# Two-layer hybrid backbone in one kernel: fewer filler matmuls in the first stage, a last block output by output, and shifted places in the order of three later parts

## The chip, the cores and the metric

The kernel runs on one core of a Trainium2 chip. The metric is the device time of one execution in microseconds (us); lower is better. The kernel before was run three times: 1451.67, 1452.0 and 1443.84 us, median 1451.67. One more execution was recorded by the profiler; all durations below come from that one.

The engines are named as in the profile: PE is TensorE (matmuls; PEld is its weight load, the step that puts the stationary operand into the array), DVE is VectorE, ACT is ScalarE, POOL is GpSimd, and SP is SyncE, which issues most of the loads. Each engine works through its own list of instructions in order and waits on semaphores for the others.

## What is computed

Two layers over 256 latent tokens and 256 context tokens of width 1024, all in float32. Each layer has a token mixer with three branches (retention, neighbourhood attention, grouped-query attention) and an MLP, both with RMS norms that are modulated by vectors computed from a conditioning input. The last layer only gives latent tokens.

```python
for l in range(DEPTH):
    last = l == DEPTH - 1
    mod_lat = (silu_c @ w_mod[l] + b_mod[l])[:, None, :]
    mod_ctx = silu_cc @ w_mod[l] + b_mod[l]
    sh1, sc1, gt1, sh2, sc2, gt2 = jnp.split(mod_lat, 6, axis=-1)
    ...
    h = rms_norm(x, g_pre_mix[l]) * (1.0 + sc1) + sh1
    hc = rms_norm(ctx, g_pre_mix[l]) * (1.0 + csc1) + csh1
    y, yc = token_mixer(h, hc, w_in[l], ...)
    x = x + gt1 * rms_norm(y, g_post_mix[l])
    h = rms_norm(x, g_pre_mlp[l]) * (1.0 + sc2) + sh2
    x = x + gt2 * rms_norm(squared_relu_mlp(h, w_mlp_in[l], w_mlp_out[l]), g_post_mlp[l])
    if not last:
        ...
```

Inside the mixer the grouped-query branch normalises each query head, so it needs the mean of the squares of every 64 query columns (`rms_norm(heads(gq, 8), q_gain)`).

## The kernel before, in words

**Precision and weight tiles.** Every product is made from three matmuls. A weight tile of 128x1024 floats arrives as `wr`. ACT rounds it to `wh` (the hi part), DVE subtracts to get `wl` (the lo part); `wsplit` (L230) does this and `mm3` (L184) issues hi by hi, hi by lo, lo by hi. The activations are split the same way into `hT` (layer input, transposed) or `u` (MLP hidden). There are three buffers each of `wr`, `wh` and `wl` (L34, L35). Functions `ahead` and `cut` (L1432 to L1451) issue loads three tiles ahead and splits two tiles ahead of the step that uses them.

**Who sets the order.** `MANUAL` is False (L26), so a scheduler sets the order of the instructions on each engine. It starts from the order in which the code issues them, which is a list of steps put together at L1371 to L1419. Only the prologue and a few marked steps are kept in program order (class `Ordered`, L61). The order on an engine is fixed at build time; on the chip nothing overtakes there.

**First stage** (`prologue`, L243). It computes the first two modulation vectors of layer 0, the normalised and transposed input `hT`, and the first projection (`rq`, `rk`; outputs `pr0` to `pr3`), for pairs of 128-row blocks called 0 to 3. Its order is a string, `PLAN` (L51), whose words `go` (L345) reads: `A00` are the matmuls on `modps` with the first weight tile of block 0, one word for each of its four tiles (`a2` for all four at once); `r` copies the row out of PSUM on ACT; `f` turns it into columns (the `pm` matmuls on PE and six small DVE steps, `sh` and `sc`); `T` and `t` are the transpositions `ph` of the input; `h` scales, shifts and splits them into `hT` (ACT, then DVE); `c` and `d` split the weight tile (ACT, DVE: `pwh`, `pwl`); `Gkm` is one of the six groups of four matmuls (over the four outputs) that block k adds; `w8` are eight filler matmuls of 128x128 zeros into `pr3`, whose result is overwritten. Ahead of all that, `init` (L277) issues `WARM` matmuls of 128x512 zeros. In the profile each of these float32 matmuls shows as two passes. The twenty `pr` tiles of 512 KB are issued on SP one after the other (L255), five to a block: tiles 0 to 3 for `A`, tile 4 for `G`. POOL copies one element of tile 14 (`late`, L262) and only then issues its own loads.

**Layer-0 MLP** (`mlp_steps`, L1220). First come projections of 256 columns (steps `m1`) for seven of the eight hidden chunks of the latent tokens (s0), mixed with the preparation of the context tokens' `hT` (`pre_steps`, L573), then the same seven for the context tokens (s1), and one projection of 512 columns for the eighth chunk. Then come eight steps of the second product (`pO`, four PSUM outputs, evicted by DVE into `z`), and the same for three more quarters. Each weight tile serves one step.

**Modulation by DVE** (`mod_dve`, L429). The other modulation vectors are summed on DVE: a tile `mr` of 128x1024 weights is loaded by POOL (two buffers), and for each stream (latent, context) one instruction `acc` multiplies it by a column and adds it up. A vector takes eight `mr` tiles, so 16 `acc` for both streams, and two finishing steps (`ahi`, `alo`, and for the gates `pg` matmuls and `G`). `weave_steps` (L1359) spreads such steps evenly between the steps of the main work. For the layer-0 MLP it takes the main steps from `MLA` = 16 to i - `MLB`, with i = 76 (the place where the last quarter is divided), L1383 to L1386: 60 fill steps over steps 16 to 65.

**Grouped-query branch** (`gq_done`, L1032). After each of four projections, ACT squares the result (`gsq`), PE sums the squares by tiny matmuls (`gqm`), DVE copies the sums (`qms`), then `rope` rotates the query. After the fourth, DVE makes the reciprocal roots. `mid` (L594) is called in the middle of a projection and runs what was put off to there. `NB2` (L33, L1391) is the number of layer-1 mixer steps that are issued between the normalisation of the context tokens and their transpositions.

Of the kernel before, what the change touches and what calls it, by code (L numbers as in the profile page):

```python
# [21 lines left out]
EPS = 1e-6  # L22
# [4 lines left out]
NS = 31  # L27
M0A = -28
M0B = -2
MLA = 16  # L30
MLB = 10
NT = 8
NB2 = 5  # L33
WR = 3  # L34
WH = 3  # L35
WLD = 3
# [11 lines left out]
END = ((0, 0), (1, 0))  # L48
ORD = ((0, 4, 5), (0, 4, 8))
FILL = (((0, 9), (9, 21), (21, 33)), ((0, 9), (7, 22), (22, 39)))  # L50
PLAN = ("A00 w8 A01 w6 T00 A02 w6 A03 r0 b0 w4 f0 T01 c0 w10 h00 d0 h01 w8 "  # L51
# [4 lines left out]
GATE = 14  # L56
PAD, PAD2, WP = 424, 272, 1152
WARM = 5


class Ordered:  # L61
# [20 lines left out]
def kernel(  # L82
# [26 lines left out]
    v_, s_, t_ = Ordered(tc, nc.vector), Ordered(tc, nc.scalar), Ordered(tc, nc.tensor)  # L109
# [18 lines left out]
    st = {}  # L128
# [16 lines left out]
    def T(name, w=512):  # L145
        return tp.tile([128, w], F32, tag="t", name=name)

    def sm(name, *shape):
        return smp.tile([128, *shape], F32, tag=name, name=name)
# [4 lines left out]
    def att(name="pa"):  # L154
        return atp.tile([128, 512], F32, tag="at", name=name)
# [4 lines left out]
    def ts(o, i, s1, s2, o0, o1):  # L160
        v_.tensor_scalar(out=o, in0=i, scalar1=s1, scalar2=s2, op0=o0, op1=o1)

    def tt(o, a, b, op):
        return v_.tensor_tensor(out=o, in0=a, in1=b, op=op)

    def stt(o, a, s, b, o0, o1):
        v_.scalar_tensor_tensor(out=o, in0=a, scalar=s, in1=b, op0=o0, op1=o1)
# [9 lines left out]
    def rsqrt(y, v, a):  # L177
        ts(y.bitcast(I32), v.bitcast(I32), -0.5, 1597463007.0, ALU.mult, ALU.add)
        for _ in range(3):
            stt(a, y, -0.5, v, ALU.mult, ALU.mult)  # L180
            tt(a, a, y, ALU.mult)
            stt(y, a, 1.5, y, ALU.add, ALU.mult)

    def mm3(ps, a, b, first, last):  # L184
        (ah, al), (bh, bl) = a, b
        t_.matmul(ps, ah, bh, start=first, stop=False)
        t_.matmul(ps, ah, bl, start=False, stop=False)
        t_.matmul(ps, al, bh, start=False, stop=last)
# [11 lines left out]
    sel = const.tile([128, 20], F32, tag="sel", name="sel")  # L200
# [42 lines left out]
    def prologue():  # L243
# [3 lines left out]
        pr = []  # L247
        M = {}
        raw, hi, rdy = {}, {}, {}
# [23 lines left out]
        def bias():  # L273
            M["b16"] = T("b16")
            nc.gpsimd.dma_start(out=M["b16"][0:16, 0:128], in_=b_mod[0, 0:2 * D].rearrange("(r n) -> r n", n=128))

        def init():  # L277

            w, zero = att("warm"), T("zero")
            v_.memset(zero, 0.0)  # L280
            for _ in range(WARM):
                t_.matmul(w, zero[:, 0:128], zero, start=True, stop=True)
# [20 lines left out]
        def early():  # L303
            for n_ in ("sh1", "sc1"):
                st[0, n_] = smp.tile([128, 8, 2], F32, tag=n_, name=n_, bufs=2)
            pr.extend(mmt(f"pr{i}") for i in range(4))
# [30 lines left out]
        def gemm(kp, u):  # L337
# [3 lines left out]
            for c in range(4):  # L341
                t_.matmul(pr[c], rdy[kp][i][:, k, 128 * c:128 * c + 128], hpair(kc, 512)[j],
                          start=(kc == 0 and u == 0), stop=(kc == 7 and u == 5))

        def go(ws):  # L345
            Ordered.on = True
            load_x(4)
            bias()
            load()
            init()  # L350
            early()
            sq = [pre_sq(0)]
            pre_xn(0, sq[0], True)
            sq.append(pre_sq(1))
            pre_xn(1, sq[1], True)
            ph, h32 = {}, {}
            for c in PLAN.split():
                o, n, m = c[0], int(c[1]), int(c[2:] or 0)
                if o == "c":
                    cast(n)  # L360
                elif o == "d":
                    cut(n)
                elif o == "A":
                    mod(n, (m,))
                elif o == "a":
                    mod(n)
                elif o == "r":
                    row(n)
                elif o == "w":
                    run_on(int(c[1:]))  # L370
                elif o == "b":
                    bias_columns()
                elif o == "T":
                    ph[n, m] = pre_tr(n, m)
                elif o == "t":
                    for s in range(2):
                        ph[n, s] = pre_tr(n, s)
                elif o == "f":
                    fin(n)
                elif o == "h":  # L380
                    for s in range(2):
                        if m == 0:
                            h32[s] = T("h32")
                        pre_h(0, 0, n, s, ph[n, s], (m,), h32[s])
                elif o == "G":
                    gemm(n, m)
            Ordered.on = False
            with tc.issue_after(st["hold"].ins), tc.issue_after(st["late"].ins):
                setup2()
            for i in range(4):  # L390
                st["qkdone"](i, pr[i])
# [165 lines left out]
    def pre_h(l, which, kp, s, pt, js=(0, 1), h32=None):  # L557
        sh, sc = ("sh1", "sc1") if which == 0 else ("sh2", "sc2")
        A, B = st[l, sc], st[l, sh]
        if h32 is None:  # L560
            h32 = T("h32")
        for j in js:
            kc = 2 * kp + j
            if s == 0:
                st["hT"][kc] = HL("hT", 256 if l and which else 512)
            h = st["hT"][kc]
            c = slice(256 * s, 256 * s + 256)
            i = slice(256 * j, 256 * j + 256)
            s_.activation(h32[:, i], pt[:, i], AF.Identity, scale=A[:, kc, s:s + 1], bias=B[:, kc, s:s + 1])
            v_.tensor_copy(h[0][:, c], h32[:, i])  # L570
            tt(h[1][:, c], h32[:, i], f(h[0][:, c]), ALU.subtract)
# [11 lines left out]
    def load_x(ntb):  # L583
        if "X" not in st:
            st["X"] = []
        for tb in range(len(st["X"]), ntb):
            X = S("X", F32)
            src = x if tb < 2 else xc
            r = 128 * (tb % 2)
            nc.sync.dma_start(out=X, in_=src[r:r + 128, :].rearrange("p (a b) -> p a b", a=2))  # L590
            st["X"].append(X)


    def mid():  # L594

        for u in st.pop("mid", ()):
            u()

    def hpair(kc, n):
        h = st["hT"][kc]  # L600
        return (h[0][:, 0:n], h[1][:, 0:n])
# [318 lines left out]
    def mixer(l):  # L920
        last = l == 1
        n = 256 if last else 512
# [109 lines left out]
        def gq_done(c):  # L1032
            def done(ps):
                if c == 0:
                    st["qms"] = smp.tile([128, 4, 8], F32, tag="qms", name="qms")
                sq = T("gsq")
                s_.activation(sq[:, 0:n], ps[:, 0:n], AF.Square)
                q = T("gq32")
                s_.activation(q[:, 0:n], ps[:, 0:n], AF.Copy, scale=gq_gain[:, 2 * l:2 * l + 1])
                pm = att("gqm")  # L1040
                for tb in range(n // 128):
                    t_.matmul(pm[:, 2 * tb:2 * tb + 2], sq[:, 128 * tb:128 * tb + 128], sel[:, 16:18], start=True, stop=True)
                v_.tensor_copy(st["qms"][:, 0:n // 128, 2 * c:2 * c + 2],
                               pm[:, 0:n // 64].rearrange("p (t e) -> p t e", e=2))
                rope(q)
                o = HL("gq", n)
                for e in range(2):
                    a, b = slice(64 * e, 64 * e + 64), slice(64 - 64 * e, 128 - 64 * e)
                    s_.copy(o[e][a], q[a, 0:n])
                    tt(o[e][b], q[a, 0:n], f(o[e][a]), ALU.subtract)  # L1050
                st.setdefault("gq", []).append(o)
                if c == 3:
                    w = n // 16
                    qm = st["qms"].rearrange("p t e -> p (t e)")
                    y, a = sm("gq_y", 4, 8), sm("gq_a", 32)
                    yf = y.rearrange("p t e -> p (t e)")
                    v_.tensor_scalar_add(out=qm[:, 0:w], in0=qm[:, 0:w], scalar1=EPS)
                    rsqrt(yf[:, 0:w], qm[:, 0:w], a[:, 0:w])
                    v_.tensor_scalar_mul(out=yf[:, 0:w], in0=yf[:, 0:w], scalar1=0.125)
                    st["qsc"] = y  # L1060
            return done

        for c in range(4):
# [310 lines left out]
    a, b = M0A, M0B  # L1374
# [7 lines left out]
    i = ml.index(None)  # L1382
    a, b = MLA, i - MLB  # L1383
    steps += ml[:a]
# [5 lines left out]
    m1_ = mixer(1)  # L1390
    steps += pc[:1] + m1_[:1 + NB2]  # L1391
    steps += pc[1:]
    steps += [([], lambda ws: st.__setitem__("X", st["X"][0:2]))]
    steps += m1_[1 + NB2:]
    steps += wout_steps(1, 0)
# [158 lines left out]
```

## Time and profile before

| what | value |
|---|---|
| runs | 1451.67, 1452.0, 1443.84 us (median 1451.67) |
| profiled execution | 1449.71 us |
| its span | 1448.0 us |
| mean granted TensorE clock | 0.995 of full speed |
| PE busy | 1420.2 us, 98% |
| DVE busy | 1049.8 us, 72% |
| ACT busy | 723.0 us, 50% |
| POOL busy | 75.7 us, 5% |
| HBM read | 217.22 MB |

The span is what the profile's engines cover; the execution's own time is 1.7 us longer. Busy shares are averages over stages that differ. A matmul's start is exact while its end is modelled, so the time that one takes in a row is best read from the start of the next. In the views, `ps<-hT,wh` means an instruction that writes a tile `ps` and reads `hT` and `wh`; the square brackets at the end of a row tell how long the engine stood idle before it and what released it. The line is L73 for nearly all, since a helper issues them, so tiles are told apart by name.

### The profile page before, as it was taken

What the parts mean: (1) busy time and instruction counts of PE and PEld (TensorE: products, weight loads), DVE (VectorE), ACT (ScalarE), POOL (GpSimd) and SP (SyncE); (2) the same over time, 40 slices, a digit from 0 to 9 for tenths busy, and PEclk for the clock granted to TensorE, in tenths of its full rate; (3) what the DMA queues carried; (4) which work ended last, traced back from release to release, by engine and by line L of the source; (5) the groups of instructions that cost most, each with busy time, mean ns of one, the idle gap of its engine ahead of it and who ended that gap; (6) DMA issues with size and microseconds to landing.
All of it is one profiled execution on the core that took longest, in us unless ns stands there. A gap on an engine that the chain in (4) does not pass through costs nothing.

```text
span 1448.0 us, 21148 instructions
## 1 busy us (share of the span) xinstructions
PE 1420.2 (98%) x8061; PEld 1206.5 (83%) x8061; DVE 1049.8 (72%) x1993; ACT 723.0 (50%) x1231; POOL 75.7 (5%) x139
## 2 busy tenths in 40 slices
PE   8999999999999999999999999999999999999997
PEld 6778788777888789988888678878889999899886
DVE  4767687777995879885855645986867886767544
ACT  3455366545322358524334144764646664487542
POOL 2000000000110000110110100000000000000000
PEclk9999899999999999999999999999999999999999
DMA  9332131222565566755673744533233446478653
GB/s 358 136 88 73 30 88 59 69 84 81 183 201 154 180 229 174 233 171 178 201 234 124 243 129 158 150 114 89 78 97 103 146 136 190 116 201 272 201 187 129
DMA packets 231862, 219.65 MB, mean 152 GB/s; under 512 B 7548, under 2 KB 188860, under 8 KB 231760
## 3 DMA queue, kind: packets, MB, share of 16 engines
q1 hardware_dynamic: 217568, 169.90, 37.8%
q0 software_dynamic: 13904, 47.88, 10.7%
q8 instruction: 63, 1.03, 0.3%
q10 hardware_dynamic: 288, 0.52, 0.1%
q14 instruction: 39, 0.32, 0.1%
HBM read 217.22 MB, written 1.05 MB: 151 GB/s over the span
## 4 chain that ended last, share of the span: by engine, by line
PE 82%; DVE 8%; DMA 5%; ACT 2%; issue 2%; SPq 0%; DVEq 0%; POOL 0%; ACTq 0%; POOLq 0%
PE ps L73 40%; PE pO L73 13%; PE br L73 7%; PE pB L73 6%; DMA mr<-in_w_mod_dram 4%; PE po L73 3%; PE pt L73 2%; DVE wl L73 2%; PE pr L73 2%; PE sl L73 2%; PE gkv L73 2%; DVE acc L73 1%; DVE hT L73 1%; PE ro L73 1%; ACT wh L73 1%
## 5 line engine op out<-in xcount | busy, mean ns | idle before, releaser
L73 PE MATMUL ps<-hT,wh 128*128 128x256 f32 (+1 forms) x2480 | 602.8, 335 | 3.5 <-DVE z L73 2.6
L73 ACT CAST wh<-wr 128x1024 fp32r<-128x1024 f32 x295 | 310.2, 1053 | 453.7 <-PE ps L73 180.6
L73 DVE TENSOR_TENSOR wl<-wr,wh 128x1024 fp32r<-128x1024 f32 x295 | 359.9, 1222 | 210.6 <-ACT wh L73 206.4
L73 PEld LDWEIGHTS ps<-hT,wh 128*128 128x128 f32 x2480 | 418.5, 190 | 58.2 <-issue 10.0
L73 PE MATMUL ps<-hT,wl 128*128 128x256 f32 (+1 forms) x1240 | 412.4, 333 | 1.1 <-DVE wl L73 1.1
L73 PEld LDWEIGHTS ps<-hT,wl 128*128 128x128 f32 x1240 | 234.2, 189 | 24.7 <-DVE wl L73 2.1
L73 PE MATMUL pO<-wh,u 128*128 128x512 f32 x768 | 239.4, 390 | 0.8 <-DVE z L73 0.8
L73 PEld LDWEIGHTS pO<-wh,u 128*128 128x128 f32 x768 | 144.2, 188 | 33.2 <-issue 2.6
L73 DVE SCALAR_TENSOR_TENSOR acc<-mr,cs,acc 128x1024 f32<-128x1024 f32 x112 | 140.7, 1281 | 32.4 <-DMA mr<-in_w_mod_dram 32.1
L73 PE MATMUL pO<-wl,u 128*128 128x512 f32 x384 | 149.6, 390 | 0.0
L73 PEld LDWEIGHTS pO<-wl,u 128*128 128x128 f32 x384 | 72.1, 188 | 14.7
L73 PE MATMUL pB<-wh,hT 128*128 128x512 f32 x256 | 82.4, 392 | 0.8 <-ACT rqk L73 0.8
L489 POOL DMA_DIRECT2D mr<-in_w_mod_dram x80 | 42.5, 531 | 426.7 <-DVE acc L73 403.8
L73 PE MATMUL pO<-wh,yT 128*128 128x512 f32 x192 | 59.7, 390 | 0.0
L73 PEld LDWEIGHTS pB<-wh,hT 128*128 128x128 f32 x256 | 48.1, 188 | 11.0 <-ACT rqk L73 1.2
L73 DVE TENSOR_TENSOR PT<-pt,PT 128x512 fp32r<-128x512 f32 x80 | 51.5, 683 | 2.4 <-ACT PT L73 1.7
L73 PE MATMUL pB<-wl,hT 128*128 128x512 f32 x128 | 50.0, 390 | 0.0
L73 ACT CAST PT<-pt 128x512 fp32r<-128x512 f32 x80 | 43.3, 599 | 8.9 <-PE pt L73 5.0
L73 DVE TENSOR_TENSOR u<-rl,u 128x256 fp32r<-128x256 f32 (+1 forms) x71 | 36.7, 518 | 12.4 <-ACT u L73 12.2
L73 PE MATMUL pt<-ident,P 128*128 128x128 f32 x320 | 41.6, 273 | 0.6 <-DVE P L73 0.6
L73 PEld LDWEIGHTS pO<-wh,yT 128*128 128x128 f32 x192 | 35.9, 188 | 7.3
L845 POOL DMA_DIRECT2D bt<-in_relb_dram x16 | 8.6, 540 | 628.7 <-DVE m L73 628.7
(273 smaller groups left out, 1849.6 us busy)
## 6 DMA issues: line engine op xcount, KB each, us to landing
wr<-in_w_m_dram SPq DMA_DIRECT2D x143, 512.0 KB, 4.4
wr<-in_w_in_dram SPq DMA_DIRECT2D x104, 512.0 KB, 3.7
mr<-in_w_mod_dram POOLq DMA_DIRECT2D x80, 512.0 KB, 4.2
wr<-in_w_br_dram SPq DMA_DIRECT2D x24, 512.0 KB, 3.5
wr<-in_w_out_dram SPq DMA_DIRECT2D x24, 512.0 KB, 4.1
pr<-in_w_mod_dram SPq DMA_DIRECT2D x16, 512.0 KB, 8.6
bt<-in_relb_dram POOLq DMA_DIRECT2D x16, 192.0 KB, 2.7
X<-in_x_dram SPq DMA_DIRECT2D x4, 512.0 KB, 4.7
```

What stands on the lines that cost most here:

```text
L73: ins = call(*a, **k)
L489: nc.gpsimd.dma_start(out=w, in_=w_mod[l, 128 * kc:128 * kc + 128, vec * D:vec * D + D].rearrange("p (a n) -> p a n", a=2))
L845: nc.gpsimd.dma_start(out=bt, in_=relb[l, h])
```

## The change

1. `PLAN`: fillers of block 0 go from 8, 6, 6, 4, 10 and 8 to 3, 2, 3, 2, none and 7 (42 to 17); `WARM` goes from 5 to 4.
2. The last three groups of block 3 become a word `L3`: the new `gemm_end` issues the same twelve matmuls output by output, so that `pr0` is complete first.
3. `MLA` goes from 16 to 8 and `MLB` from 10 to 6: the weave of the layer-0 MLP covers the main steps 8 to 69.
4. `NB2` goes from 5 to 6.
5. The square sums of the grouped-query branch (`gqm` matmuls, the copy into `qms`, after the fourth the roots) become a function `sums`, which the next call of `mid` runs.

```diff
-MLA = 16
-MLB = 10
+MLA = 8
+MLB = 6
 NT = 8
-NB2 = 5
+NB2 = 6
...
-PLAN = ("A00 w8 A01 w6 T00 A02 w6 A03 r0 b0 w4 f0 T01 c0 w10 h00 d0 h01 w8 "
+PLAN = ("A00 w3 A01 w2 T00 A02 w3 A03 r0 b0 w2 f0 T01 c0 h00 d0 h01 w7 "
...
-        "G30 G31 G32 G33 G34 G35")
+        "G30 G31 G32 L3")
...
-WARM = 5
+WARM = 4
...
+        def gemm_end(kp):
+
+            for c in range(4):
+                w = [x[:, 1, 128 * c:128 * c + 128] for x in rdy[kp]]
+                mm3(pr[c], w, hpair(2 * kp + 1, 512), False, True)
...
+                elif o == "L":
+                    gemm_end(n)
...
-        for u in st.pop("mid", ()):
+        for u in st.pop("late_mm", []) + list(st.pop("mid", ())):
             u()
...
-                pm = att("gqm")
-                for tb in range(n // 128):
-                    t_.matmul(pm[:, 2 * tb:2 * tb + 2], sq[:, 128 * tb:128 * tb + 128], sel[:, 16:18], start=True, stop=True)
-                v_.tensor_copy(st["qms"][:, 0:n // 128, 2 * c:2 * c + 2],
-                               pm[:, 0:n // 64].rearrange("p (t e) -> p t e", e=2))
                 rope(q)
...
+                def sums():
+                    pm = att("gqm")
...
+                st.setdefault("late_mm", []).append(sums)
```

What stands in an engine's list, place by place. First PE at the start of the kernel, before:

```order
L73 MATMUL warm<-zero 128x512 x5
L73 MATMUL modps<-pr,csz 32x256 x4
L73 MATMUL pr_192<-csz 128x128 x8
L73 MATMUL modps<-pr,csz 32x256 x4
L73 MATMUL pr_192<-csz 128x128 x6
L73 MATMUL ph<-ident,X 128x128 x4
L73 MATMUL modps<-pr,csz 32x256 x4
L73 MATMUL pr_192<-csz 128x128 x6
L73 MATMUL modps<-pr,csz 32x256 x4
L73 MATMUL pr_191<-ident,b_129 128x16
L73 MATMUL pr_192<-csz 128x128 x4
L73 MATMUL pm<-csz,r_283 128x2 x4
```

And of the change:

```order
L73 MATMUL warm<-zero 128x512 x4
L73 MATMUL modps<-pr,csz 32x256 x4
L73 MATMUL pr_191<-csz 128x128 x3
L73 MATMUL modps<-pr,csz 32x256 x4
L73 MATMUL pr_191<-csz 128x128 x2
L73 MATMUL ph<-ident,X 128x128 x4
L73 MATMUL modps<-pr,csz 32x256 x4
L73 MATMUL pr_191<-csz 128x128 x3
L73 MATMUL modps<-pr,csz 32x256 x4
L73 MATMUL pr_190<-ident,b_129 128x16
L73 MATMUL pr_191<-csz 128x128 x2
L73 MATMUL pm<-csz,r_270 128x2 x4
```

The row `pr<-csz` is a run of fillers. Each run is shorter, and the rows between stand in the same order.

Next DVE in the layer-0 MLP, from the first weight split after the last `hT` of the context tokens. `acc<-mr` is a modulation sum, `wl<-wr,wh` a weight split, `u<-rl` a split of the hidden activations. Before:

```order
L73 TENSOR_TENSOR wl_5633<-wr_5594,wh_5632 128x1024
L73 TENSOR_TENSOR u_5563<-rl_5589,u_5563 128x256
L73 TENSOR_TENSOR wl_5669<-wr_5630,wh_5668 128x1024
L73 TENSOR_TENSOR u_5293<-rl_5625,u_5293 128x256
L73 SCALAR_TENSOR_TENSOR acc_5779<-mr_5774,cs_103,brow_5776 128x1024
L73 TENSOR_TENSOR u_5330<-rl_5661,u_5330 128x256
L73 TENSOR_TENSOR wl_5705<-wr_5666,wh_5704 128x1024
L73 SCALAR_TENSOR_TENSOR acc_5781<-mr_5774,cs_103,brow_5776 128x1024
L73 TENSOR_TENSOR wl_5741<-wr_5702,wh_5740 128x1024
L73 TENSOR_TENSOR u_5367<-rl_5697,u_5367 128x256
L73 SCALAR_TENSOR_TENSOR acc_5779<-mr_5819,cs_103,acc_5779 128x1024
L73 TENSOR_TENSOR wl_5786<-wr_5738,wh_5785 128x1024
```

And of the change:

```order
L73 TENSOR_TENSOR wl_5628<-wr_5585,wh_5627 128x1024
L73 SCALAR_TENSOR_TENSOR acc_5524<-mr_5519,cs_103,brow_5521 128x1024
L73 SCALAR_TENSOR_TENSOR acc_5526<-mr_5519,cs_103,brow_5521 128x1024
L73 SCALAR_TENSOR_TENSOR acc_5524<-mr_5540,cs_103,acc_5524 128x1024
L73 SCALAR_TENSOR_TENSOR acc_5526<-mr_5540,cs_103,acc_5526 128x1024
L73 TENSOR_TENSOR u_5550<-rl_5576,u_5550 128x256
L73 TENSOR_TENSOR u_5267<-rl_5616,u_5267 128x256
L73 TENSOR_TENSOR u_5304<-rl_5656,u_5304 128x256
L73 TENSOR_TENSOR wl_5668<-wr_5625,wh_5667 128x1024
L73 SCALAR_TENSOR_TENSOR acc_5524<-mr_5581,cs_103,acc_5524 128x1024
L73 SCALAR_TENSOR_TENSOR acc_5526<-mr_5581,cs_103,acc_5526 128x1024
L73 SCALAR_TENSOR_TENSOR acc_5524<-mr_5621,cs_103,acc_5524 128x1024
```

Before, one `acc` at most stands between two `wl`; with the change four `acc` stand there, from the first `wl` on, for three tiles running (the third four follow after the last row shown here, then two, `u` and two).

Last PE in the same stretch. `ps<-hT,wh` and `ps<-hT,wl` are matmuls of a projection with the hi and the lo part of its weight tile. Before, at the end of one projection and the beginning of the next:

```order
L73 MATMUL ps_5708<-hT_5062,wh_5668 128x256 x2
L73 MATMUL ps_5708<-hT_5062,wl_5669 128x256
L73 MATMUL ps_5708<-hT_5066,wh_5668 128x256 x2
L73 MATMUL ps_5708<-hT_5066,wl_5669 128x256
L73 MATMUL ps_5744<-hT_5020,wh_5704 128x256 x2
L73 MATMUL ps_5744<-hT_5020,wl_5705 128x256
L73 MATMUL ps_5744<-hT_5024,wh_5704 128x256 x2
L73 MATMUL ps_5744<-hT_5024,wl_5705 128x256
```

And of the change, at the end of the projection that uses the first `wl` above:

```order
L73 MATMUL ps_5671<-hT_5040,wl_5628 128x256
L73 MATMUL ps_5711<-hT_4994,wh_5667 128x256 x2
L73 MATMUL ps_5751<-hT_4994,wh_5707 128x256 x2
L73 MATMUL ps_5791<-hT_4994,wh_5747 128x256 x2
L73 MATMUL ps_5711<-hT_4994,wl_5668 128x256
L73 MATMUL ps_5711<-hT_4998,wh_5667 128x256 x2
L73 MATMUL ps_5711<-hT_4998,wl_5668 128x256
L73 MATMUL ps_5711<-hT_5008,wh_5667 128x256 x2
```

With the change PE issues the first two hi matmuls of three projections before the first matmul that needs the second `wl`; the rest of each projection stands behind it in PE's order. On SP the order is the same in both; in layer 1 the projection issued ahead by `NB2` stands on PE where it stood.

## Rows read from the trace of the kernel before

**Rows 1.** The page, part 1: engine, busy us (share of the span), instructions.
```profile
PE 1420.2 (98%) x8061; PEld 1206.5 (83%) x8061; DVE 1049.8 (72%) x1993; ACT 723.0 (50%) x1231; POOL 75.7 (5%) x139
```

**Rows 2.** What PE waited for over the span: us in total, times, longest.
```profile
PE warm L73 <- DVE zero L73: 3.7, 1, 3.7
PE ph L73 <- ACT z L73: 3.3, 3, 1.6
PE ps L73 <- DVE z L73: 2.6, 2, 2.4
...
PE ps L73 <- DVE wl L73: 1.1, 2, 0.7
PE pO L73 <- DVE z L73: 0.8, 2, 0.5
...
PE pB L73 <- ACT rqk L73: 0.8, 1, 0.8
```

**Rows 3.** Busy time by engine (x instructions), PEclk, DMA share, GB/s, 582.3 to 596.6 us.
```profile
582.30:596.60 14.30, 14.30 (x121) 14.30 (x121) 12.43 (x14) 9.57 (x17) 1.08 (x2) 1.00 0.81 241
```

**Rows 4.** Timeline, 0 to 50 us: start us, us, engine, line, operation [idle before <- releaser].
```profile
8.11 0.34 PEld L73 LDWEIGHTS warm<-zero 128*128 128x128 f32 x1 [0.52 <-issue]
...
9.44 0.19 PEld L73 LDWEIGHTS warm<-zero 128*128 128x128 f32 x1 [0.24 <-issue]
...
11.20 0.64 PE L73 MATMUL modps<-pr,csz 128*32 128x256 f32 x8 [0.31 <-DVE pv L73]
...
11.77 2.05 PE L73 MATMUL pr<-csz 128*128 128x128 f32 x16
...
18.40 0.64 PE L73 MATMUL modps<-pr,csz 128*32 128x256 f32 x8
...
20.12 0.95 PE L73 MATMUL pm<-csz,r 128*128 128x2 f32 x8
...
21.40 4.18 PE L73 MATMUL pr<-csz 128*128 128x128 f32 x36
...
23.22 0.43 DVE L73 TENSOR_TENSOR hT<-h,hT 128x256 fp32r<-128x256 f32 x1
...
25.34 2.09 PE L73 MATMUL pr<-hT,pwh 128*128 128x512 f32 x8
...
30.65 0.18 POOL L262 COPY late<-pr 128x1 f32<-128x1 f32 x1 [27.16 <-DMA pr<-in_w_in_dram]
...
45.95 1.93 PE L73 MATMUL modps<-pr,csz 128*32 128x256 f32 x32
```

**Rows 5.** Timeline of DVE, 585 to 597 us.
```profile
586.16 1.28 DVE L73 SCALAR_TENSOR_TENSOR acc<-mr,cs,brow 128x1024 f32<-128x1024 f32 x1
587.36 1.22 DVE L73 TENSOR_TENSOR wl<-wr,wh 128x1024 fp32r<-128x1024 f32 x1
588.49 0.42 DVE L73 TENSOR_TENSOR u<-rl,u 128x256 fp32r<-128x256 f32 x1
588.83 1.28 DVE L73 SCALAR_TENSOR_TENSOR acc<-mr,cs,acc 128x1024 f32<-128x1024 f32 x1
```

**Rows 6.** Tile `mr`, 580 to 630 us: its last line.
```profile
DMA to landing us min/median/max: 3.8/4.3/7.2
```

**Rows 7.** Timeline of PE, 596 to 597 us.
```profile
596.75 0.63 PE L73 MATMUL ps<-hT,wh 128*128 128x512 f32 x2
```

**Rows 8.** Timeline of DVE, 802 to 805 us.
```profile
802.26 1.29 DVE L73 SCALAR_TENSOR_TENSOR acc<-mr,cs,acc 128x1024 f32<-128x1024 f32 x1 [2.66 <-DMA mr<-in_w_mod_dram]
...
804.60 1.28 DVE L73 TENSOR_TENSOR z<-z,pO 128x512 f32<-128x512 f32 x2
```

**Rows 9.** Busy time by engine, 140 to 168 us, columns as in rows 3.
```profile
140.00:144.00 4.00, 4.00 (x22) 3.49 (x22) 3.83 (x7) 3.76 (x7) 0.00 (x0) 0.77 0.00 0
...
160.00:164.00 4.00, 4.00 (x15) 3.42 (x15) 1.37 (x6) 1.28 (x3) 0.00 (x0) 0.50 0.00 0
164.00:168.00 4.00, 4.00 (x13) 2.57 (x12) 2.41 (x6) 0.21 (x1) 0.00 (x0) 0.74 0.00 0
```

More of the change, by code (lines that the diff above doesn't have):

```diff
@@ L1051, in done @@
                 st.setdefault("gq", []).append(o)
[L1052 to L1060, printed above, removed]
+                def sums():
+                    pm = att("gqm")
+                    for tb in range(n // 128):
+                        t_.matmul(pm[:, 2 * tb:2 * tb + 2], sq[:, 128 * tb:128 * tb + 128], sel[:, 16:18], start=True, stop=True)
+                    v_.tensor_copy(st["qms"][:, 0:n // 128, 2 * c:2 * c + 2],
+                                   pm[:, 0:n // 64].rearrange("p (t e) -> p t e", e=2))
+                    if c == 3:
+                        w = n // 16
+                        qm = st["qms"].rearrange("p t e -> p (t e)")
+                        y, a = sm("gq_y", 4, 8), sm("gq_a", 32)
+                        yf = y.rearrange("p t e -> p (t e)")
+                        v_.tensor_scalar_add(out=qm[:, 0:w], in0=qm[:, 0:w], scalar1=EPS)
+                        rsqrt(yf[:, 0:w], qm[:, 0:w], a[:, 0:w])
+                        v_.tensor_scalar_mul(out=yf[:, 0:w], in0=yf[:, 0:w], scalar1=0.125)
+                        st["qsc"] = y
+                st.setdefault("late_mm", []).append(sums)
             return done
```

## The prediction, made before the changed kernel ran

> **What bounds the kernel now.** I read the page's busy times first. PE is busy for 1420.2 of 1448.0 us [rows 1], so at most 28 us of its idle time can be won, and anything further has to come from PE doing less work. The table of what PE waited for [rows 2] breaks the idle time up: 3.7 us before the first matmul, and no other wait above 3.3 us in total. VectorE (DVE) is the second engine, at 72%. That is an average, and the reader should look at the stretch where the weave of the layer-0 MLP begins: from 582.3 to 596.6 PE is busy 14.30 of 14.30 us and DVE 12.43 [rows 3]. There DVE has 1.9 us to spare in 14.3, and it serves PE: every weight tile needs a `wl` from DVE before its projection can run. So I read the change in two places: the first stage, where PE loses work, and the beginning of that weave, where DVE gains work.
>
> **First stage, step by step.** Ten warm passes end at 10.89, and the first `modps` matmul (A00) starts at 11.20 [rows 4]. A00 needs the first `pr` tile, so one warm matmul less (two passes) only lengthens PE's idle time ahead of it. I count it at nothing. From there the 16 fillers' passes last from 11.77 to A01 at 13.75, and the 36 passes of w10 and w8 from 21.40 to G00 at 25.34 [rows 4]: 0.25 and 0.22 us a filler (two passes each). Fewer fillers bring the next A forward only if its tile is there. The first tile lands near 11.15, and the fifteenth releases POOL's `late` copy at 30.65 [rows 4], so tiles land (30.65 - 11.15)/14 = 1.39 us apart. After the change A01 starts at 12.55 (tile), A02 at 14.1 (after two fillers and the transposes T00), A03 at 15.4 (tile 15.3; three fillers end there) against 18.40: 3.0 us earlier. The chain from A03 to G00 goes over ACT's row copy, the `pm` matmuls (20.12) and the scaling on ACT. With two fillers fewer ahead of `pm` it moves by 3.4. G00 also needs `hT` from DVE; the fourth `hT` step starts at 23.22 [rows 4], 3.1 us after `pm`, and the hi parts that G00 reads are done just then; after the change that is 19.8. Seven fillers after the transposes end at 19.5. G00 therefore starts near 19.8: 5.6 us gained. If the gap between tiles were longer here, the gain would be about 4; the ceiling is the 25 fillers by 0.23, or 5.8 us. Later tiles are not late: the nineteenth lands at 11.15 + 18 x 1.39 = 36.2, and its use at 45.95 [rows 4] moves to 40.3. The last block output by output lets `pr0` end nine matmuls (2 us) earlier, so the `rqk` evictions no longer hold up the first `pB` matmul: 0.8 us [rows 2]. Sum: -6.4, between -4 and -7.5.
>
> **Beginning of the MLP weave.** This is the largest term. The weave now starts at step 8, not 16, so eight more steps of modulation sums come before the weight splits in program order. DVE works strictly in its order. In the rows of before one or two `acc` stand between two `wl`; now four do, for three tiles running, then two and two. I replay both engines with the durations of before. Starts of successive rows give 1.14 us for a `wl`, 1.20 for an `acc`, 0.34 for a `u` [rows 5]. The `mr` buffers are two, and a new tile lands 4.3 us after issue in this stretch [rows 6]; with 0.3 us for the release, an estimate, I take 4.6. The first two tiles are there already, because the buffers have long been free. The first `wl` of the stretch ends at 580.1 as before, and its projection runs on PE from 582.35 to 585.2: the 512-column projection starts at 596.75 [rows 7], and five 256-column ones of 2.88 us (24 matmuls of 0.12) lie ahead of it.
> DVE: four `acc` to 584.9, three `u` and a `wl` to 587.1. The next pair of `acc` needs the tile requested at 582.5, ready 587.1; so four `acc`, `u`, `wl` to 593.4. The next four wait 0.7 us for `mr`, `wl` at 600.4. Again the same, `wl` at 607.4; then `u`, two `alo` and the `wl` of the 512-column projection at 611.2.
> PE: before each wait it can run only the leading hi matmuls that the order shows, 0.24 us a projection. It waits 1.2 us for the second `wl` (585.9 to 587.1), then 3.4, 3.9, 3.9 for the next three, and about 0.5 for the last, since six `pg` matmuls lie in between. Sum 13 us. Before, the same stretch has no PE idle at all [rows 3], so all of this is new. The lower bound has no `mr` wait, so rounds of 6.3 us (four `acc`, a `u`, a `wl`) instead of 7.0: 12. Upper bound: the longest landing of the stretch, 7.2 us [rows 6], adds 2.9 us in each of three rounds: 22. I take 13, since the median landing is from this very place.
>
> **The rest of the weave.** Sixty fill steps now lie over 62 main steps, before over 50, so DVE's order is looser afterwards. In before DVE stands in `acc`, waiting for `mr`, with the evictions `z` queued behind it (802.26, then `z` at 804.60) [rows 8], and PE waits 2.6 us in `ps` and 0.8 in `pO` for `z` [rows 2]. I expect these to go: -3 (bounds 0 and -3.4; what comes next is late by less, `wl` 1.1 us in two waits).
>
> **Layer 1.** With NB2 at 6 PE's order there stays as it was; ACT does the scaling `z` earlier, and two `ph` waits (3.3 us in total [rows 2]) shrink: -0.8, between -3 and +2, since the put-off square sums also move `rope` steps ahead of `hT` on DVE. In layer 0 putting them off leaves PE's order unchanged.
>
> **Clock.** The granted clock falls to 0.77 after 140 us, and to 0.50 and 0.74 after 160 [rows 9], 4 us lost in these three slices. PE's matmuls there come in the same order; only their start moves by 6 us. I count it at 0, plus or minus 4; one of the three runs of before is 8 us under the others.
>
> **Sum.** The profiled execution took 1449.7 us, 1.7 more than its span and 2 less than the median of the three runs. 1449.7 - 6.4 + 13 - 3 - 0.8 = 1452.5. The gain of the first stage is given back in the weave.
>
> **Rivals.** (1) `mr` tiles land late. The DMA engines are busy for a share of 0.81 from 582 to 597 [rows 3], so a tile can be held up. With 7.2 us the weave costs 22, so 1461, slower than before; it decides over the forecast from a landing of about 6 us. For it: the 7.2 itself. Against: a median of 4.3.
> (2) The order does not starve PE, because DVE's queue gets ahead of PE before 580 by more than I see. Then PE's work alone counts: 1449.7 - 6.4 - 3 - 0.8 = 1439.5. For it: PE has been the bound everywhere [rows 1]. Against: the fourth `wl` has 12 `acc` and 5 `u` ahead of it, 16 us of work, and DVE has 1.9 us spare. The Trainium skill's page "Perfetto Trace Analysis", section "Identifying the Most-Contended Engine", says to optimise the engine with the highest occupancy first, and by the share of 98% that is PE here; by that rule the time would be the 1439.5 of this rival. The stretch of rows 3 speaks against using it for the whole span.
> (3) Fewer matmuls leave PE slow at the start. Weight loads take 0.34 us to 8.11 and 0.19 from 9.44 on [rows 4]: PE changes from its 1.2 GHz durations to the 2.4 GHz ones after about eight passes. If it falls back in the new gap before A00, a fall like the longer one on record (0.50 and 0.74 over 4 us each [rows 9]) loses 3.0 us: 1455.5. For it: the added idle time. Against: eight passes remain. The Trainium skill's "TensorE: Matmul & The Clock Gate", section "What's actually happening", says that the default state is throttled and activity releases it, which speaks against taking out fillers; no row here shows the clock falling in this stage, and by the rule the time would be this rival's.
> (4) The fillers only covered waits: the chain over ACT and DVE, not PE's queue, sets G00. Gain 0 to 1, so 1458.
>
> **How the numbers follow.** Forecast 0.55; rival 1 0.15; rival 2 0.15; rival 3 0.08; rival 4 0.07. One per cent is about what a measurement of this kernel can tell from no change: 1437.2 to 1466.2 around the median 1451.7. The forecast's own range is 1446 to 1461. With the clock's 4 us either way, rival 2 reaches under 1437 in about half of its chance, giving 0.1 faster with a little from the forecast; rival 1 and the forecast's upper end together give 0.14 slower; 0.76 same. The range 1440 to 1466 leaves out the far halves of rivals 1 and 2.
>
> **What would show it.** In the changed profile: G00 near 19.8, A03 near 15.4, and no `pB` wait for `rqk`; a new line "PE ps <- DVE wl" of about 13 us in four or five waits between 580 and 612 (on before's clock), DVE almost without idle time there, waiting only for `mr`; the 512-column projection ending near 610 (616 on before's clock, less 6). The waits of PE for `z` gone. No `wl` wait there would mean rival 2; waits of 5 us or more each, rival 1; weight loads of 0.34 us after 11 us, rival 3; G00 at 24 or later, rival 4.

## The result, and the profile after

The changed kernel took 1455.97 us in the median of 20 runs, the kernel before 1449.03 us in the median of 20 runs beside it: ratio 1.0053, interval 1.0039 to 1.0066 (the two medians alone give 1.0048). It is slower by 0.5%, inside one per cent. The prediction was 1452.5 us. The profiled execution took 1452.4 us (span 1450.2), at the low end of the runs.

The page of the changed kernel, its busy times and the granted clock in 40 slices:

```profile
PE 1417.4 (98%) x8009; PEld 1201.6 (83%) x8009; DVE 1048.9 (72%) x1993; ACT 722.9 (50%) x1231; POOL 76.0 (5%) x139
...
PE   8999999999999999799999999989999999999997
...
PEclk9999999999999999899999999999999999999999
```

PE is busy 2.8 us less than in [rows 1], and its share is again 98%. That is not the work of the 26 matmuls left out alone, since in both kernels time that a matmul takes at a lowered clock counts as busy too. By these shares nothing has happened. One slice, at 580 to 616 us, has a 7 in PE's row and an 8 in the clock; that is the stretch of the weave.

The same matmuls can be found in both traces, and the difference of their starts tells where time came and went:

| place (start of the same matmul, us) | before | after | difference |
|---|---|---|---|
| first `pB` | 60.59 | 54.32 | -6.3 |
| `rmt`, layer 0 | 154.84 | 148.19 | -6.7 |
| first `gqm` after the early falls of the clock | 171.02 | 161.27 | -9.8 |
| first 256-column projection of the MLP | 554.4 | 544.4 | -9.9 |
| its eleventh, where the weave's waits begin | 585.23 | 577.57 | -7.7 |
| 121st matmul of `pO`, first quarter | 631.3 | 638.5 | +7.2 |
| projection after that quarter's `pO` | 738.43 | 747.20 | +8.8 |
| `ph`, layer 1 | 915.73 | 921.00 | +5.3 |
| `warm`, layer 1 | 1249.40 | 1254.87 | +5.5 |
| `pO`, layer 1 | 1352.15 | 1354.41 | +2.3 |

**First stage.** PE's timeline of the changed kernel, 0 to 62 us (start, duration, operation, idle before):

```profile
10.89 0.64 PE L73 MATMUL modps<-pr,csz 128*32 128x256 f32 x8 [0.54 <-DVE pv L73]
...
15.41 0.64 PE L73 MATMUL modps<-pr,csz 128*32 128x256 f32 x8
...
19.98 2.11 PE L73 MATMUL pr<-hT,pwh 128*128 128x512 f32 x8
...
54.32 0.39 PE L73 MATMUL pB<-wh,hT 128*128 128x512 f32 x1
```

And the first `pB` matmul before:

```profile
60.59 0.50 PE L73 MATMUL pB<-wh,hT 128*128 128x512 f32 x1 [0.77 <-ACT rqk L73]
```

The rows of the change are A00, A03, the first `G` group and the first `pB` matmul, to be held against [rows 4]: A03 3.0 us earlier, `G` 5.4, `pB` 6.3, and no idle time ahead of `pB`. A00 itself is 0.3 us earlier, so from A00 to `pB` the gain is 6.0.

**Beginning of the weave.** What PE waited for in 560 to 620 us (us in total, times, longest):

```profile
PE ps L73 <- ACT wh L73: 5.6, 3, 3.0
PE pO L73 <- ACT wh L73: 1.9, 1, 1.9
PE ps L73 <- DVE wl L73: 0.7, 2, 0.4
PE pg L73 <- ACT ahi L73: 0.4, 1, 0.4
...
```

Before, PE did not idle in the stretch of [rows 3]. Most of the new waits are named after ACT's `wh`, not DVE's `wl`. DVE's timeline shows what stands behind them:

```profile
571.33 1.21 DVE L73 TENSOR_TENSOR wl<-wr,wh 128x1024 fp32r<-128x1024 f32 x1
572.47 2.46 DVE L73 SCALAR_TENSOR_TENSOR acc<-mr,cs,brow 128x1024 f32<-128x1024 f32 x2
574.86 2.46 DVE L73 SCALAR_TENSOR_TENSOR acc<-mr,cs,acc 128x1024 f32<-128x1024 f32 x2
577.25 1.08 DVE L73 TENSOR_TENSOR u<-rl,u 128x256 fp32r<-128x256 f32 x3
578.26 1.21 DVE L73 TENSOR_TENSOR wl<-wr,wh 128x1024 fp32r<-128x1024 f32 x1
579.54 4.87 DVE L73 SCALAR_TENSOR_TENSOR acc<-mr,cs,acc 128x1024 f32<-128x1024 f32 x4
...
584.67 1.22 DVE L73 TENSOR_TENSOR wl<-wr,wh 128x1024 fp32r<-128x1024 f32 x1
586.70 2.48 DVE L73 SCALAR_TENSOR_TENSOR acc<-mr,cs,acc 128x1024 f32<-128x1024 f32 x2 [0.82 <-DMA mr<-in_w_mod_dram]
...
592.27 1.22 DVE L73 TENSOR_TENSOR wl<-wr,wh 128x1024 fp32r<-128x1024 f32 x1
...
599.03 1.22 DVE L73 TENSOR_TENSOR wl<-wr,wh 128x1024 fp32r<-128x1024 f32 x1
```

Four sums, three `u`, a `wl`; four sums, a `u`, a `wl`: the order shown ahead of the prediction, almost without a gap up to 586 us. After that DVE waits for `mr` three times, 1.6 us in all. ACT's timeline tells why its `wh` is late:

```profile
584.28 1.04 ACT L73 CAST wh<-wr 128x1024 fp32r<-128x1024 f32 x1 [0.99 <-DMA wr<-in_w_m_dram]
...
590.37 0.38 ACT L73 ACTIVATE rl<-ps 128x256 f32<-128x256 f32 x1 [4.74 <-PE ps L73]
...
591.30 1.04 ACT L73 CAST wh<-wr 128x1024 fp32r<-128x1024 f32 x1
...
597.90 0.38 ACT L73 ACTIVATE rl<-ps 128x256 f32<-128x256 f32 x1 [5.25 <-PE ps L73]
...
598.64 1.04 ACT L73 CAST wh<-wr 128x1024 fp32r<-128x1024 f32 x1
```

In ACT's list the `wh` stands behind `rl`, the first step of the projection before, and that waits 4.7 and 5.3 us for PE, which waited for DVE's `wl`. So one late `wl` holds up the projection that needs it, then the next tile's `wh`, and with it PE's next hi matmuls. (The `wh` at 584.28 also waited 1.0 us for its own load.) PE's timeline there:

```profile
585.38 0.50 PE L73 MATMUL ps<-hT,wh 128*128 128x256 f32 x2 [2.96 <-ACT wh L73]
585.94 0.38 PE L73 MATMUL ps<-hT,wl 128*128 128x256 f32 x1
...
592.39 0.73 PE L73 MATMUL ps<-hT,wh 128*128 128x512 f32 x2 [2.06 <-ACT wh L73]
593.55 0.58 PE L73 MATMUL ps<-hT,wl 128*128 128x256 f32 x1 [0.42 <-DVE wl L73]
...
599.73 0.82 PE L73 MATMUL pO<-wh,u 128*128 128x512 f32 x2 [1.87 <-ACT wh L73]
600.99 1.22 PE L73 MATMUL pg<-ahi,ones 128*128 128x512 f32 x2 [0.43 <-ACT ahi L73]
602.01 0.41 PE L73 MATMUL ps<-hT,wl 128*128 128x256 f32 x1
...
611.74 0.39 PE L73 MATMUL pO<-wl,u 128*128 128x512 f32 x1
```

At 585.94 and 593.55 PE goes on 0.05 us after the `wl` that it needs (585.89 and 593.49 on DVE), so an earlier `wh` alone would not have freed it. The stop ahead of 599.73 is not for a projection: the order has the first two `pO` matmuls and two `pg` matmuls ahead of the projection that the fifth `wl` (ready at 600.25) would have let run; that starts at 602.01, 1.8 us after its `wl`. And the granted clock:

```profile
584.00:588.00 4.00, 2.56 (x14) 2.36 (x15) 3.18 (x5) 1.35 (x2) 0.53 (x1) 0.82 0.71 224
588.00:592.00 4.00, 2.33 (x12) 2.12 (x11) 3.64 (x4) 1.50 (x3) 0.53 (x1) 0.75 0.81 233
592.00:596.00 4.00, 3.19 (x13) 2.75 (x14) 4.00 (x6) 0.65 (x2) 0.53 (x1) 0.67 0.63 198
596.00:600.00 4.00, 2.13 (x14) 1.93 (x13) 3.58 (x4) 2.06 (x5) 1.11 (x3) 0.90 0.74 248
600.00:604.00 4.00, 3.57 (x15) 2.85 (x15) 3.62 (x5) 1.88 (x2) 2.47 (x4) 0.57 0.76 211
```

The column after POOL's is PEclk: PE is at half speed (1.2 GHz) for parts of this stretch, in three falls of 3.4 us (from 586.6, 593.4 and 600.2) that follow its idle times.

### The profile page after: what moved, and what is told of

The parts are those of the page before. It is cut to its first block, busy times and chain, and to the rows that moved or that the text cites. A ratio compares the mean times of both kernels' runs of the same rounds, so it can differ in the third digit from the quotient of the medians.

```text
span 1450.2 us, 21045 instructions
## 1 busy us (share of the span) xinstructions
PE 1417.4 (98%) x8009; PEld 1201.6 (83%) x8009; DVE 1048.9 (72%) x1993; ACT 722.9 (50%) x1231; POOL 76.0 (5%) x139
## 3 DMA queue, kind: packets, MB, share of 16 engines
q0 software_dynamic: 13904, 47.88, 10.6%
HBM read 217.22 MB, written 1.05 MB: 151 GB/s over the span
## 4 chain that ended last, share of the span: by engine, by line
PE 80%; DVE 9%; issue 5%; DMA 3%; ACT 2%; POOL 0%; DVEq 0%; SPq 0%; ACTq 0%; POOLq 0%
PE ps L73 36%; PE pO L73 16%; PE br L73 7%; PE pB L73 6%; PE po L73 3%; PE pt L73 2%; DVE wl L73 2%; DMA mr<-in_w_mod_dram 2%; PE sl L73 2%; PE pr L73 2%; PE gkv L73 2%; DVE acc L73 1%; DVE hT L73 1%; PE ro L73 1%; ACT wh L73 1%
## 5 line engine op out<-in xcount | busy, mean ns | idle before, releaser
L73 PE MATMUL ps<-hT,wh 128*128 128x256 f32 (+1 forms) x2480 | 602.7, 335 | 8.2 <-ACT wh L73 5.6
L73 PEld LDWEIGHTS pO<-wl,u 128*128 128x128 f32 x384 | 72.1, 188 | 14.5
L73 DVE TENSOR_SCALAR P<-P,su 128x512 f32<-128x512 f32 (+1 forms) x96 | 40.3, 440 | 1.6
```

What stands on the lines that cost most here:

```text
L73: ins = call(*a, **k)
```

## The experiments

Each was timed beside the kernel before; ratios are to it, with their interval. "The change" stands at 1.0053.

**1. The change with the old weave.**

```diff
-MLA = 8
-MLB = 6
+MLA = 16
+MLB = 10
```

> The changed kernel with the weave of the layer-0 MLP put back (MLA 16, MLB 10), all else as changed. Theory (the weave costs 18 us where it begins, in PE waits and in a lowered clock, and gives 3.4 back later): 1456.0 - 18 + 3.4 = about 1441, 8 us under before; no PE wait for `wh` or `wl` near 580 to 605 us and no fall of the clock there. Rival (the put-off square sums or NB2 carry the loss): 1452 or more.

Measured 1447.85 us, ratio 0.9971 (0.9952 to 0.999). In its trace PE waits 0.2 us between 556 and 625, and the clock does not fall there. The weave thus makes the difference of 0.8% (12 us) between this kernel and the change, less than the 14.6 expected. By its ratio the kernel is 4 us under before, where the theory has 8; the rival, which is at or above before, lies outside the interval. Its profiled execution lost more to the early falls of the clock (13.7 us at half speed at 151 us, against 3.4 in the change's).

**2. The weave alone on the kernel before.**

```diff
-MLA = 16
-MLB = 10
+MLA = 8
+MLB = 6
```

> The kernel before with MLA 8 and MLB 6 alone. Theory: 1449.0 + 18 - 3.4 = about 1463.5, with 9 us of PE waits and two or three falls of the clock between 585 and 620 us. Rival (the weave alone is harmless, the loss needs the other edits): within 3 us of before, 1449.

Measured 1461.24 us, ratio 1.0073 (1.0049 to 1.0097): 10.6 us lost, where 14.5 were expected, with the other edits out of play. PE's waits between 556 and 625 us:

```profile
PE ps L73 <- ACT wh L73: 5.0, 3, 2.6
PE pO L73 <- ACT wh L73: 1.9, 1, 1.9
...
```

The same waits in nearly the same sizes, and three falls of the clock. The weave alone carries the loss.

**3. The first stage alone on the kernel before** (`PLAN`, `WARM` and `gemm_end` as in the change).

> The kernel before with the first stage of the change alone (PLAN, WARM, last block output by output). Theory: the 6.3 us that the first pB matmul starts earlier are kept to the end: 1449.0 - 6.3 = 1442.7. Rival (the gain is given back in the next stages, or the clock falls more often after a shorter first stage): 1447 or more.

Measured 1445.71 us, ratio 0.9962 (0.9943 to 0.9981): 5.5 us gained, between theory and rival and within 1 us of the theory. In its profile the whole gain stands from 98 to 155 us (6.6), and 17 us of lowered clock between 135 and 166 take 3.1 of it back; this one execution is worse there than that of before.

**4. NB2 and the put-off sums alone on the kernel before.**

> The kernel before with NB2 at 6 and the square sums put off, nothing else. Theory: worth 1 us at most either way, 1447.5 to 1450. Rival (the put-off sums cost in layer 1, or the other way they take the early falls of the clock away): 3 us or more off 1449, upward in the first case, downward in the second.

Measured 1450.12 us, ratio 1.0002 (0.9987 to 1.0017). Nothing, as expected.

**5. Narrow sums.** Fourteen of the first sixteen sums are cut to 8 columns, so most of that vector is left out (`stt` issues the instruction `acc`).

```diff
-                    stt(a, w, cs[:, kc, s:s + 1], M["b"] if kc == 0 else a, ALU.mult, ALU.add)
+                    if (l, vec) == (0, 5) and kc:
+                        stt(a[:, 0, 0:8], w[:, 0, 0:8], cs[:, kc, s:s + 1], a[:, 0, 0:8], ALU.mult, ALU.add)
+                    else:
+                        stt(a, w, cs[:, kc, s:s + 1], M["b"] if kc == 0 else a, ALU.mult, ALU.add)
```

> The changed kernel, but of the 16 sums of the first vector in the weave (the second gate of layer 0) 14 work on 8 columns and not on 1024, so most of that vector is left out; every mr tile is still loaded and waited for. Theory (DVE's time in these sums starves PE): the PE waits between 575 and 615 us fall from 8.6 to 4 or less, the clock falls there at most once, and the time is 1456 - 12 or more, near 1442. Rival (the landing of the mr tiles sets the pace, DVE's work is beside the point): waits of 7 us or more stay, 1453 or more.

Measured 1449.0 us, ratio 1.0004 (0.9986 to 1.0023): 7 us below the change, where 14 were expected. PE's timeline of 575 to 612 us has one idle time:

```profile
593.00 1.22 PE L73 MATMUL pg<-ahi,ones 128*128 128x512 f32 x2 [6.08 <-ACT ahi L73]
```

All waits of the projections are gone, so DVE's work in the sums made those. In their place PE stands 6.1 us before `pg`, which needs the finished vector: with DVE's work taken out, DVE waits 6.6 us for `mr` in five waits (1.6 in the change), so the eight `mr` tiles through two buffers are what is late. Theory and rival were both half right. The two limits lie one behind the other, close together.

**6. PE kept busy in its waits.** 33 matmuls whose result is not used.

```diff
                 ps = mmt()[:, k]
+                if l == 0 and q == 0 and streams == (1,) and c >= 3:
+                    d = att("fill")
+                    for _ in range(10 if c > 3 else 3):
+                        t_.matmul(d[:, 0:512], ones, st["hT"][0][0], start=True, stop=True)
```

> The changed kernel with 33 matmuls of 128x512, whose result is not used, put on PE before the four projections that wait (3, 10, 10, 10); DVE's order is as in the changed kernel. 33 x 0.227 = 7.5 us of filling for 8.6 us of waits. Theory (the lowered clock in the waits' wake adds to the loss, since PE ends up behind DVE): no fall of the clock between 575 and 615, the named PE waits under 3 us, and 2 to 4 us less than the changed kernel, 1452 to 1454. Rival (DVE alone sets the pace, PE's clock there costs nothing): 1455 to 1458.

Measured 1455.75 us, ratio 1.0051 (1.0031 to 1.0071), the change's own. The rival holds by the time. Its busy times in the stretch:

```profile
584.00:588.00 4.00, 4.00 (x23) 3.41 (x22) 4.00 (x5) 2.16 (x4) 1.06 (x2) 1.00 0.85 243
588.00:592.00 4.00, 4.00 (x31) 3.72 (x30) 2.60 (x3) 0.80 (x2) 0.00 (x0) 1.00 0.82 251
592.00:596.00 4.00, 3.12 (x14) 2.07 (x12) 3.92 (x5) 1.35 (x2) 1.05 (x2) 1.00 0.52 149
596.00:600.00 4.00, 2.90 (x22) 2.69 (x22) 3.69 (x5) 0.80 (x2) 0.53 (x1) 1.00 0.80 258
600.00:604.00 4.00, 1.37 (x3) 0.80 (x4) 3.55 (x5) 2.85 (x4) 2.15 (x4) 0.84 0.59 174
```

The clock stays at 1.00 up to 600 us and falls once, not three times. PE's idle time is 4.7 us and not 8.6; most of what is left is one wait of 3.3 us of `pO` for `wh`. Still the stretch loses as much: from -5.3 at the first of the added matmuls to +9.7 at the 121st `pO` matmul, 15.0 us, against 14.9. The second to fifth `wl` end 6.3, 7.9 and 6.7 us apart, in the change 6.4, 7.6 and 6.8. So DVE's list sets the pace, and PE at half speed between the first waits loses only time that it would have waited. The last fall of the clock is in both kernels (from 602.7 here, from 600.2 in the change), so what that one costs is not tested.

**7. A later start, a looser end** (MLA 16, MLB 6, all else as changed).

> The changed kernel with MLA 16 and MLB 6: the weave begins where it did before and ends four steps later (60 fill steps over 54). Theory (the loss comes from the early start, the gain from the looser end): no wait near 580 to 610, and PE's waits for z shorter than before, 1443 to 1447, at or under the run with the old weave (1447.9). Rival (the looseness was not what took the z waits away): like the old weave, 1448 or more.

Measured 1442.61 us, ratio 0.9954 (0.9937 to 0.997): the lowest ratio of the study, clear of before and of the change. Its interval overlaps those of (1) and (3), so a gain over the old weave is not shown. Against the change only the start differs: starting at step 8 costs 14 us. No wait of PE above 0.2 us between 556 and 625. Its waits from 625 to 935 us:

```profile
PE ps L73 <- DVE z L73: 2.1, 1, 2.1
PE ps L73 <- DVE wl L73: 0.4, 1, 0.4
...
```

Only one wait for DVE's `z` is left, where before had 2.6 and 0.8 us [rows 2] and the old weave 3.5 and 0.3.

**8. Start halfway** (MLA 12, MLB 6).

> The changed kernel with MLA 12 and MLB 6: start halfway. In DVE's order two or three sums stand between two wl where the changed kernel has four. Theory (what decides is DVE's work between two wl, 2.5 sums x 1.2 + 1.14 + 0.34 = 4.5 us against PE's 2.88 us a projection): waits of 3 to 6 us, 1447 to 1452, between old weave and change. Rival (only bunches of four starve PE): no waits, 1446 or less.

Measured 1450.77 us, ratio 1.0006 (0.9986 to 1.0025). PE's waits between 556 and 625 us:

```profile
PE ps L73 <- ACT wh L73: 3.4, 2, 2.8
PE ps L73 <- DVE wl L73: 1.4, 1, 1.4
...
```

4.8 us in the named waits, in the range of the theory, and so is the time: two to three sums between two `wl` starve PE too, by less.

**9 and 10. Both kernels again, for second profiles.**

> The changed kernel unchanged, for a second profile. Theory (the pace of layer 1's 256-column projections, 113 ns a matmul in the changed kernel's profile against 118 before, is set anew in each execution): 118 may show; the time is then 3 us above that profile's 1452.4. Rival (the pace belongs to the program): 113 again. In both the waits between 575 and 612 us stay at 8 to 9 us, and the weave loses 14 to 16 us against before between the two ends of it.

> The kernel before unchanged, for a second profile. The falls of the clock between 135 and 170 us (10.2 us at half speed in the first profile): theory (they move from one execution to the next): another sum or another place; rival (they belong to the order of PE's work): 10 us at the same places. The pace in layer 1's MLP: 118 by the rival of the run before, either by its theory.

The change measured 1458.72 us, ratio 1.0058 (1.0029 to 1.0086), before 1449.17, ratio 1.0001 (0.9979 to 1.0023). The pace of layer 1's projections was 113 ns again in the change and 118 again in before, so it belongs to the program. PE's idle time between 575 and 612 us was 8.5 us again in the change, and the stretch lost 14.8 us against before, as expected. In before the fall of the clock at 142 us (3.4 us) came again, and the longer one at 159 us did not: 3.4 us and not 10.2 in all, so those falls differ between executions. And the change's second profile shows something new in the first stage. PE's timeline and busy times:

```profile
3.57 5.28 PE L73 MATMUL warm<-zero 128*128 128x512 f32 x8 [3.57 <-DVE zero L73]
11.94 0.64 PE L73 MATMUL modps<-pr,csz 128*32 128x256 f32 x8 [3.09 <-DVE pv L73]
```

```profile
8.00:12.00 4.00, 0.91 (x6) 0.11 (x9) 2.94 (x16) 2.30 (x4) 0.00 (x0) 1.00 1.04 375
12.00:16.00 4.00, 4.00 (x30) 2.67 (x30) 2.85 (x15) 0.00 (x0) 0.00 (x0) 0.70 1.08 393
16.00:20.00 4.00, 4.00 (x35) 2.40 (x33) 0.24 (x2) 1.28 (x2) 0.00 (x0) 0.87 1.09 385
```

Here the eight warm passes took 5.28 us (6.69 in the first profile) and ended at 8.85, and A00 started 1.05 us later; the gap ahead of A00 grew to 3.1 us, and the clock then fell to 0.70 and 0.87 in the next two slices. The first `pB` came at 56.91 and not at 54.32, 2.6 us later. The late A00 makes 1.05 of it; the other 1.5 were lost after A00, with the fall of the clock.

**11 and 12. Two more places for the weave** (MLA 16 and MLB 2; MLA 24 and MLB 2).

> The changed kernel with MLA 16 and MLB 2: same beginning as before, 58 main steps. Theory (a late start keeps the projections fed, a looser end takes z waits away): no waits of PE at 575 to 612, less than 2 us of waits for z, 1440 to 1444. Rival (the sums of the last vectors then collide with the last quarter's evictions or come too late for layer 1): 1446 or more.

> The changed kernel with MLA 24 and MLB 2: the weave begins only in the second product, where PE takes 5.4 us a weight tile against 2.9. Theory (the projections of 256 columns are the one place where DVE cannot carry sums): 1439 to 1444. Rival (60 steps over 50 crowd the rest as in before, z waits of 3 us or more): 1445 to 1448.

Measured 1445.73 us, ratio 0.9985 (0.9963 to 1.0006), and 1451.84 us, ratio 1.0016 (0.9997 to 1.0034). Both theories missed. Neither kernel has PE waits of note at 575 to 612, but in 800 to 900 us the first has a wait of 3.3 us of `pO` for `wl`, the second 2.6 us of `pO` for `wh` and 2.0 for `z` and `wl`. That sums put further back crowd the last quarter's product would explain them; it is not shown. Each profile also has 10 us of lowered clock between 940 and 1007 us, which the experiments do not explain.

## Why the prediction came out as it did

**The direction and the mechanism were right.** The first stage gains, the bunches of sums at the weave's new beginning give it back and more. Undoing the weave (1), the weave alone (2), half of it (8), a later start (7) and taking DVE's work out (5) all say so. From the eleventh projection to the 121st `pO` matmul PE takes 46.1 us in every profile with the weave from step 16 to 65 or 69 (before twice, 1, 3, 4, 7), 60.9 and 60.8 in the change, 61.3 in (2), 53.7 in (8) and 54.3 in (5). By their ratios the weave (2), the first stage (3) and the rest (4) alone make +10.6, -5.5 and +0.3 us, together 5.4; the change makes 7.7 (5.7 to 9.6).

**The number: partly luck.** The sum is 2.8 us above the profile of before. The first pair of profiles differs by 2.7 us, the second pair by 12.0 (1458.72 and 1446.69), the medians by 6.9. In the first pair terms that the sum did not have cancel: 2.3 us lost ahead of the weave, 1.9 more than forecast in its beginning and 1.6 behind it, against 3.1 from the early falls of the clock and 3.2 from layer 1's MLP.

**First stage: right.** Forecast -6.4; -6.3 at the first `pB`, and -5.5 alone (3). A03 came at 15.41 (forecast 15.4), the first `G` at 19.98 (19.8). From A00 to `pB` the four profiles with the old first stage take 49.4 or 49.5 us, and nine of the ten with the new one 43.4, a gain of 6.0. A00 itself comes at 10.8 to 11.2 us with the old and at 10.5 to 11.9 with the new. But 2.3 us of PE's lead were lost before the weave, between the first and the eleventh projection of the MLP: PE's weight loads now wait five times, 1.6 us, for `hT` (0.3 before). PE is 9.9 us ahead of before there, and DVE's last `hT` only 7.6 (570.66 against 578.30). With the old weave (1) 1.6 us go there too. This term was not in the sum.

**Beginning of the weave: mechanism right, size short.** DVE's replay held: its `wl` were ready at 579.5, 585.9, 593.5 and 600.3, forecast (less the 7.6 us by which DVE's stretch starts earlier) 579.5, 585.8, 592.8 and 599.8. Its waits for `mr` came to 1.6 us, forecast 1.4. PE's side held up to the fifth `wl`. Its idle time was 8.6 us, but its projections that start at 585.94 and 593.55 took 4.4 and 4.3 us at the lowered clock, where 22 matmuls of 0.12 make 2.6; idle time and the added 3.4 us together are 12.0, forecast 12.4 in four waits. That is why the waits look smaller than what was lost: time at half speed is busy time in the profile. (6) shows that the first two falls of the clock were no cost of their own.

The step that failed is the last one: "before each wait it can run only the leading hi matmuls that the order shows", and with it "about 0.5 for the last, since six `pg` matmuls lie in between". Those six do lie in between (605.36 to 606.75), and the last wait was nothing. But ahead of the projection with the fifth `wl` PE's order has two more `pg` and two `pO` matmuls, which themselves wait for `ahi` and `wh`. They fell on the path, not into a wait, and the projection started 1.8 us after its `wl`; its 22 matmuls took 3.3 us, since the clock was low again. So the 512-column projection ended at 611.74, where the replay's 616, moved by 7.6, has 608.4. Of these 3.3 us, 0.5 is DVE's later `wl`, 1.8 PE's order and 0.7 the clock in that projection (an estimate from these rows). The stretch lost 14.9 us and not 13.

The clock fell three times in the change's stretch, each time behind an idle time of 1.9 to 3.0 us; (6) has one fall, behind its one long wait of 3.3 us. The Trainium skill's "TensorE: Matmul & The Clock Gate", section "What's actually happening", says that activity releases a throttle that is otherwise on; these falls agree with it.

**The rest of the weave: right, but not all.** From 738 to 916 us 3.5 us came back (forecast 3); before that, from 631 to 738, 1.6 were lost, of which 0.9 in two new waits of `pO` for `z`.

**Layer 1: the waits right, the stage not.** The waits of `ph` for `z`, three and not the two that the prediction counts, shrank from 3.3 to 2.4 us (forecast 0.8 less), and alone the edits are worth nothing (4). One `gqm` wait shrank too (1.7 to 0.2 us), but a new wait of 1.2 us for `hT` and a fall of the clock at 1006 us stand against that, and from 916 to 1249 us nothing is won (+5.3 to +5.5). Not foreseen: 3.2 us in layer 1's MLP, below.

**Clock: a draw that fell both ways.** Forecast 0, plus or minus 4. In the first pair of profiles the early falls favour the change by 3.1 us, in the second pair they do not (6.8 us at half speed in the change, 3.4 in before). Such draws, and the first-stage fall of (9), can make the 2.7 us of the first pair out of the 6.9 of the medians; that they do is not shown.

**The rivals.** Rival 2 (no starvation, 1439.5) is refuted by the waits. Rival 1 (late `mr` tiles) is a limit just behind the first, as (5) shows, but in the change landings were 4.1 us in the median, 4.7 at most. Rival 3 (PE slow at the start) was dismissed too quickly: it shows in one of the ten profiles that have the new first stage, and costs 1.5 us there, not 3.0. Rival 4 (the fillers only covered waits) is refuted by (3).

## What to carry to other kernels

Where side work is spread over an in-order engine that also feeds the bottleneck, compare its work per feed with the bottleneck's time per feed, stretch by stretch: four sums, a `u` and a `wl` take 6.3 us against 2.9 us of a projection; by the same count the second product, with 24 matmuls of 0.227 us or 5.4 us per tile, would carry two or three sums (an estimate). Starting this weave eight steps earlier cost 14 us, 1.0% ((7) against the change); with the start as before, the other edits were worth 0.5%. A replay of the feeding engine's list predicted its times to within a microsecond here; on the fed engine everything that its order puts in front of the waiting work must be counted as well, other waits included.

## What was not expected of the hardware

The 256-column projections of layer 1's MLP ran at two paces, at a listed clock of 1.00. Busy times of 1288 to 1304 us, before and after:

```profile
1288.00:1304.00 16.00, 16.00 (x139) 16.00 (x138) 11.94 (x14) 12.16 (x24) 1.08 (x2) 1.00 0.73 205
```

```profile
1288.00:1304.00 16.00, 16.00 (x144) 16.00 (x143) 10.48 (x14) 12.76 (x24) 0.00 (x0) 1.00 0.70 200
```

139 matmuls in 16 us against 144 (medians of the starts 118 and 113 ns), worth 3.2 us over the stage. Repeats gave the same pace for the same kernel; of the others 1, 6 and 12 had 113, the rest 118. The order of PE's work there is the same in both; what sets the pace was not tried.

Filling PE's waits with matmuls kept its clock up for most of the stretch and won nothing (6), and after a shorter warm-up the clock can fall in the wake of the gap that it leaves (9, in one profile of ten). The length of an idle time does not tell by itself: 2.3 us ahead of A00 in (1) were followed by no fall, 1.9 us in the weave of the change by one.
